# Encoder layer on one core: the first sequence's matrix-memory blocks are turned by VectorE and a DRAM buffer instead of by TensorE

## The chip, the core and the metric

The program runs on one core of a Trainium2 chip. The metric is the device time of one execution in microseconds (us). Five engines work side by side, each through its own instructions strictly in the order in which they stand: TensorE (PE, with PEld for its weight loads), VectorE (DVE), ScalarE (ACT), GpSimd (POOL) and SyncE (SP). DMA transfers are issued by instructions that stand in the queue of SP, POOL or ACT, and an instruction that waits holds up everything behind it on its engine.

## The reference, cut to what matters

Two sequences of 512 tokens (`x_prompt`, here s = 0, and `x_sample`, s = 1) go through the same layer: a half-step SwiGLU feed-forward, a mixing block, a second feed-forward, a final norm. In the mixing block a grouped-query attention (8 heads) and a bidirectional matrix memory (4 heads of width 128) run on the same normalised input:

```
att = gqa_block_attention(aq, ak, av)
mem = mlstm_bidirectional(mq, mk, mv, gate_pre, mlstm_gate_bias, o_pre, mlstm_head_norm)
merged = sigmoid(g_att) * (att @ w_up_att) + sigmoid(g_mlstm) * (mem @ w_up_mlstm)
x = x + merged @ w_out
```

Each direction of the memory computes, per head, weights from the gates, multiplies them with the scores `q k`, divides by the larger of the row sum's magnitude and `exp(-m)`, and applies the result to `v`; the two directions are added, normalised per head and gated.

## The kernel before, in words

Everything is kept transposed (128 channels on the partitions, 512 tokens along the row). Products are made in float32 precision from two parts of each operand: `split` writes a rounded high part (ACT, L733) and the rest (DVE, L734), and a product is three passes (high x high, high x low, low x high). Weights are split in the same way when they are first used: `load_w` fetches a raw tile `wr` (SP queue, L277), ACT writes the high part `w` (L284), DVE the low part (L285), and SP stores both into DRAM (`wpark`, L309). The second sequence loads the parked parts (L299) and splits nothing.

`mix(s, ...)` is the mixing block; both sequences run it one after the other, with parts interleaved. Units of work are pairs (load, compute), and `go` issues a unit's load one unit (s = 0) or two units (s = 1) ahead of the oldest one held. A scheduler then places the instructions on each engine by priority and by its own estimate of when each could run; `pin` keeps an instruction in program order, and `mark` pins the last matmul of a unit while `marks[0]` is set. So the order on an engine is not the order of the source.

The places the change and the prediction touch:

- Attention's end: `score` (L1118), softmax, `turn_keys` (PE transposes, L1134) or `fetch` of turned blocks from DRAM, `values` (L1165). Products of other units stand between them on PE.
- `mem_values`: the projection of the memory's `v` (96 products of 512 columns, L821), from four weight tiles, into the three banks `mm` and the bank `pso`.
- `mem_rows(h, d)`: loads the gate row of head h and direction d, spread over all partitions, into a quarter-tile `eb` of the tile `box` (L1088), and adds the mask to it to make `em` (L1091).
- `mem_head(h)`: four score products (L1309; the banks `pss`, two of them), 20 exponentials of 128x128 on ACT (L1323), DVE's product with row sums (L1325), the reciprocal `dn` (L1329 to L1331), and the normalisation (ACT L1336, DVE L1337 and L1339).
- `mem_out(h, ...)`: the four normalised tiles have to be turned so that they can be multiplied with `v` (L1381). The second sequence does this without PE: `mem_blocks` turns 32x32 blocks on DVE (L1347; eight instructions a head into two tiles `qt`), `mem_send` writes them to the DRAM buffer `tbuf` in eight DMAs on POOL's queue (L1355), and `mem_out` reads four tiles `f` back (L1368). The first sequence turns them by PE: 16 transposes of 128x128 a head (L1372) into the banks `pst`. Behind the product comes the head's norm (`block_sums`, `block_rstd` with its PE product L238, `spread_rows`).
- `merge_att(d)` (products with `w_up_att`), `mem_gate(d)`, `att_gate(d)` (gate projections): the units that stand between the heads.
- Small pools: four raw weight tiles `wr`, four row tiles `f2` (names `f`), eleven tiles `t2` (names `t`).

Of the kernel before, what the change touches and what calls it, by code (L numbers as in the profile page):

```python
# [8 lines left out]
F32 = mybir.dt.float32  # L9
# [3 lines left out]
ALU = mybir.AluOpType  # L13
# [3 lines left out]
P = 128  # L17
S = 512
D = 1024
KD = D // P  # L20
# [6 lines left out]
def encoder(ctx, tc, I, outs):  # L27
    nc = tc.nc
# [3 lines left out]
    wpool = ctx.enter_context(tc.tile_pool(name="wpool", bufs=3))  # L32
# [9 lines left out]
    def nm(s):  # L42
        n_id[0] += 1
        return f"{s}_{n_id[0]}"
# [269 lines left out]
    V_ = nc.vector  # L314
    G_ = nc.gpsimd
# [422 lines left out]
    HM, DM = 4, 128  # L738
# [8 lines left out]
    tabs = []  # L747
# [39 lines left out]
    marks = [False]  # L787
# [4 lines left out]
    def go(*units):  # L792
        for load, comp in units:
            held.append((comp, load()))
            while len(held) > ahead[0]:
                c, w = held.pop(0)
                c(w)
# [65 lines left out]
    EARLY = 6  # L863

    def mix(s, xh, xl, early=None, extra=None, after=None):
# [3 lines left out]
        queue = []  # L869

        def fill(n):
            go(*queue[:n])
            del queue[:n]

        def F2(dtype=F32):
            return T2(dtype, "f2")
# [52 lines left out]
        mg = A([P, KD, S], F32, "mg")  # L929
# [39 lines left out]
        ebuf = dpool.tile([2, 4, HM, P], F32, name=nm("ebuf"))  # L969
# [52 lines left out]
        def mem_values():  # L1022
            def done(pvv):
                vm = A([P, 2, 4, S], F32R, "Vm")
                for b in range(4):
                    nc.scalar.activation(vm[:, 0, b, :], pvv[b], AF.Copy, scale=rcol(b))
                    rest(vm[:, 1, b, :], pvv[b], b, f(vm[:, 0, b, :]))
                Vm.append(vm)
            return tok_proj(xh, xl, [(1792, 512)], 2, done, (MM, MM, MM, PO))
# [3 lines left out]
        def mem_qk(h, j):  # L1033
            def done(pp):
                if j == 0 and not s:
                    t = wpool.tile([P, 4, S], F32R, tag="w8", bufs=4, name=nm("qk"))
                    qks[h] = [t[:, i] for i in range(4)]
                elif s:
                    t = mem[:, 2 + j] if h == 2 else wpool.tile([P, 2, S], F32R, tag="wr", bufs=4, name=nm("qk"))
                    qks.setdefault(h, []).extend(t[:, i] for i in range(2))  # L1040
                t = pp
                if not s:
                    t = F2()
                    V_.tensor_tensor(t, pp, R[s], op=ALU.mult)
                split(t, *qks[h][2 * j:2 * j + 2])
            return win_cols((768, 1280)[j] + h * P, done)
# [10 lines left out]
        def att_gate(d):  # L1057
            def done(pp):
                gate_of(mg[:, d, :], pp)
            return win_cols(2832 + d * P, done)  # L1060
# [23 lines left out]
        def mem_rows(h, d):  # L1084

            eb = T2(F32, "eb")
            eb3 = eb.rearrange("p (b s) -> p b s", b=4)
            nc.sync.dma_start(eb3, ebuf[d, :, h, :].partition_broadcast(P))  # L1088
            em = T2(F32, "eb")
            em3 = em.rearrange("p (b s) -> p b s", b=4)  # L1090
            (V_ if s or not h else G_).tensor_tensor(em3, eb3, tabs[3][:, d].unsqueeze(1).to_broadcast([P, 4, P]), op=ALU.add)  # L1091
            return eb3, em3

        def mem_scales():
# [178 lines left out]
        def merge_att(d):  # L1273
            def done(pu):
                V_.scalar_tensor_tensor(mg[:, d, :], mg[:, d, :], 1.0, pu, op0=ALU.add, op1=ALU.mult)
            return up_unit(0, d, att, done)
# [3 lines left out]
        def mem_gate(d):  # L1280
            def done(pp):
                t = ths[d] = T2()
                gate_of(t, pp)
            return win_cols(3856 + d * P, done)
# [56 lines left out]

        def mem_blocks(h, Ts):

            q = [wpool.tile([P, 8, 4, 32], F32, tag="wr", bufs=4, name=nm("qt")) for _ in range(2)]
            for i in range(4):
                for g in range(2):
                    V_.transpose(q[g][:, :, i, :],  # L1347
                                 Ts[i][0][:, g * 256:(g + 1) * 256].rearrange("p (n m) -> p n m", m=32))
            return h, q

        def mem_send(h, q):

            for g in range(2):
                for a in range(4):
                    mark(nc.gpsimd.dma_start(tbuf[h % 2][8 * g:8 * g + 8, :, a, :].rearrange("n r x -> r n x"),  # L1355
                                      q[g][32 * a:32 * a + 32].rearrange("r n i m -> r n (i m)")), True)
            return h % 2

        def mem_out(h, Ts):
            moved = isinstance(Ts, int)  # L1360
            vm = Vm[0]
            po = PO()
            hs_ = slice(h * P, (h + 1) * P)
            turned = []
            for j in range(4 + 1):
                if j < 4 and moved:
                    p = F2()
                    mark(nc.gpsimd.dma_start(p, tbuf[Ts][4 * j:4 * j + 4].rearrange("c r a x -> (c r) (a x)")), True)  # L1368
                elif j < 4:
                    p = PT()  # L1370
                    for i in range(4):
                        nc.tensor.transpose(p[:, i * P:(i + 1) * P], Ts[i][0][:, j * P:(j + 1) * P], ident)  # L1372
                if j < 4:
                    ph, pl = T2(F32R), T2(F32R)
                    split(p, ph, pl)
                    turned.append((j, ph, pl))
                if j >= 1:
                    t, ph, pl = turned.pop(0)
                    with shifted(15):
                        for n, (a, b) in enumerate(((0, ph), (1, ph), (0, pl))):  # L1380
                            mark(nc.tensor.matmul(po, vm[:, a, t, hs_], b, start=(t == 0 and n == 0),  # L1381
                                                  stop=(t == 3 and n == 2)), True)
            h2 = T2()
            og = ogs[h]
            if moved:
                rows_ = T2()
                nc.scalar.activation(rows_.rearrange("p (i a m) -> p i a m", i=4, a=4),
                                     po.rearrange("p (a i m) -> p i a m", i=4, a=4), AF.Copy)
                po = rows_
            nc.scalar.activation(h2, po, AF.Square)  # L1390
            V_.scalar_tensor_tensor(og, og, 1.0, po, op0=ALU.add, op1=ALU.mult)
            turned_ = own[0] if own else F2()
            row = block_sums(h2, turned_)
            with shifted(60):
                rh = block_rstd(row, DM)
            with shifted(160):
                Rh = spread_rows(rh, turned_)
                V_.scalar_tensor_tensor(og, og, hn[:, h:h + 1], Rh, op0=ALU.mult, op1=ALU.mult)
                split(og, mem[:, h, 0, :], mem[:, h, 1, :])

        if s:
            qk2, qk3 = [[mem_qk(h, j) for j in range(2)] for h in (2, 3)]
            ma = [merge_att(d) for d in range(KD)]
            marks[0] = True
            q = mem_blocks(0, mem_head(0))
            at = [mem_send(*q)]
            go(*mem_values(), *qk2)
            q = mem_blocks(1, mem_head(1))
            go(*qk3, ma[0], ma[1])
            mem_out(0, at[0])  # L1410
            at.append(mem_send(*q))
            q = mem_blocks(2, mem_head(2))
            go(att_gate(6), att_gate(7), ma[2], ma[3])
            mem_out(1, at[1])
            at.append(mem_send(*q))
            q = mem_blocks(3, mem_head(3))
            go(*ma[4:])
            mem_out(2, at[2])
            at.append(mem_send(*q))
            go(*[mem_gate(d) for d in range(EARLY)])  # L1420
            mem_out(3, at[3])
            marks[0] = False
        for h in range(HM if not s else 0):
            Ts = mem_head(h)
            if h == 0:
                go(*mem_values())
            queue.append(merge_att(2 * h))
            if h == 0:
                queue.append(merge_att(1))
            fill(1 + s)  # L1430
            mem_out(h, Ts)
            if h + 2 < HM:
                queue.extend([att_gate(h + 6), mem_qk(h + 2, 0), mem_qk(h + 2, 1)])
            if h:
                queue.append(merge_att(2 * h + 1))
            fill(99)

        mh, ml = A([P, KD, S], F32R, "mh"), A([P, KD, S], F32R, "ml")
        go(*[mem_gate(d) for d in range(EARLY * s, KD)])
        go(*[merge_mem(d) for d in range(KD)])  # L1440
        flush()
        yield None
# [553 lines left out]
```

## Time and profile before

| what | value |
|---|---|
| time, median of 3 runs (lowest to highest) | 2029.29 us (2028.79 to 2030.15) |
| the profiled execution's own time | 2029.24 us |
| its span in the profile | 2027.5 us |
| PE busy | 2015.1 us, 99% |
| DVE, ACT, POOL busy | 1592.6, 919.2, 249.7 us (79%, 45%, 12%) |
| first sequence's attention tail, memory and merge | about 788 to 985 us from the span's start |
| second sequence's | about 1150 to 1340 us |

The span is the profiled part of the execution; the 1.7 us by which the execution's time exceeds it lie outside. An engine's share counts the time in which at least one of its instructions runs. The share of a whole span is an average; the stage from 788 us on is the one to read here.

### The profile page before, as it was taken

The numbers are of one execution on the slowest core, as the hardware profiler recorded it, in microseconds if no ns is written. First come the engines' busy times: TensorE is split into PE (matmuls) and PEld (weight loads), VectorE is DVE, ScalarE is ACT, GpSimd is POOL, SyncE is SP. The second block draws the span as 40 slices with busy tenths as digits, with TensorE's granted clock in tenths as the row PEclk, the third lists the DMA queues.
The fourth block names the chain that finished last, engine by engine and source line by source line (L and its number), as shares of the span: only waits on it lengthen the run. The fifth ranks groups of instructions, "written<-read, shape, count | busy, mean of one in ns | idle before, by whom it ended". The sixth has DMA issues, their size and how long they took to land.

```text
span 2027.5 us, 26874 instructions
## 1 busy us (share of the span) xinstructions
PE 2015.1 (99%) x9129; PEld 1661.4 (82%) x9129; DVE 1592.6 (79%) x2830; ACT 919.2 (45%) x1677; POOL 249.7 (12%) x313
## 2 busy tenths in 40 slices
PE   9999999999999999999999999999999999999998
PEld 7888888888888888788888878888888888888887
DVE  8989898896688788786566867377798988786797
ACT  7644444443224477653325655245444444442224
POOL 0243344201003000100120023011000000000001
PEclk9999999999999999999999999999999999999999
DMA  9778787799766766868657668867565655699753
GB/s 313 233 235 271 228 279 244 258 337 373 264 220 220 274 194 198 267 206 300 210 165 220 205 228 264 274 208 238 157 210 171 226 168 178 204 339 349 272 194 120
DMA packets 329546, 482.11 MB, mean 238 GB/s; under 512 B 23016, under 2 KB 196160, under 8 KB 328128
## 3 DMA queue, kind: packets, MB, share of 16 engines
q1 hardware_dynamic: 316352, 439.27, 64.9%
q0 software_dynamic: 12896, 40.86, 5.9%
q8 instruction: 72, 1.18, 0.2%
q14 instruction: 66, 0.54, 0.1%
q10 hardware_dynamic: 160, 0.27, 0.0%
HBM read 308.70 MB, written 171.61 MB: 237 GB/s over the span
## 4 chain that ended last, share of the span: by engine, by line
PE 94%; DVE 2%; DMA 2%; issue 1%; ACT 1%; SPq 0%; DVEq 0%; ACTq 0%
PE mm L856 16%; PE mm L380 11%; PE pso L380 11%; PE pst L380 11%; PE mm L650 9%; PE mm L842 5%; PE pss L380 5%; PE pss L650 4%; PE pst L650 4%; PE mm L821 3%; PE pso L650 3%; PE pss L1118 1%; PE pso L1165 1%; PE pso L1381 1%; PE pst L856 1%; PE pss L856 1%
## 5 line engine op out<-in xcount | busy, mean ns | idle before, releaser
L380 PE MATMUL pst<-xc,w 128*128 128x512 f32 x1056 | 253.8, 389 | 0.5 <-ACT t L415 0.5
L380 PEld LDWEIGHTS pst<-xc,w 128*128 128x128 f32 x1056 | 198.1, 188 | 42.0 <-ACT t L415 0.9
L380 PE MATMUL mm<-xc,w 128*128 128x512 f32 x972 | 229.8, 390 | 0.8 <-ACT t L388 0.8
L380 PEld LDWEIGHTS mm<-xc,w 128*128 128x128 f32 x972 | 181.8, 188 | 39.5 <-ACT t L388 1.9
L650 PE MATMUL mm<-rt,w 128*128 128x512 f32 x765 | 178.7, 389 | 0.0
L856 PE MATMUL mm<-xh,w 128*128 128x512 f32 x560 | 176.0, 391 | 0.0
L650 PEld LDWEIGHTS mm<-rt,w 128*128 128x128 f32 x765 | 143.5, 188 | 29.8
L338 ACT ACTIVATE w<-t 128x512 fp32r<-128x512 f32 x176 | 107.6, 628 | 130.7 <-issue 59.1
L339 DVE TENSOR_TENSOR w<-t,w 128x512 fp32r<-128x512 f32 x176 | 120.2, 701 | 31.7 <-ACT w L338 30.0
L380 PE MATMUL pso<-xc,f 128*128 128x512 f32 x528 | 127.1, 390 | 0.1
L380 PE MATMUL pss<-xc,w 128*128 128x512 f32 x528 | 126.8, 389 | 0.0
L380 PE MATMUL pso<-xc,w 128*128 128x512 f32 x528 | 126.8, 389 | 0.0
L856 PEld LDWEIGHTS mm<-xh,w 128*128 128x128 f32 x560 | 104.9, 188 | 21.8
L380 PEld LDWEIGHTS pso<-xc,f 128*128 128x128 f32 x528 | 98.9, 188 | 21.5 <-DVE t L419 1.1
L380 PEld LDWEIGHTS pss<-xc,w 128*128 128x128 f32 x528 | 99.1, 188 | 20.6
L380 PEld LDWEIGHTS pso<-xc,w 128*128 128x128 f32 x528 | 99.1, 188 | 20.6
L842 PE MATMUL mm<-xh,w 128*128 128x512 f32 x336 | 110.5, 395 | 0.0
L856 PE MATMUL mm<-xl,w 128*128 128x512 f32 x280 | 109.6, 391 | 0.0
L733 ACT ACTIVATE w<-wr 128x512 fp32r<-128x512 f32 x72 | 45.1, 632 | 138.3 <-PE pso L650 70.6
L733 ACT ACTIVATE w<-t 128x512 fp32r<-128x512 f32 x82 | 51.8, 632 | 107.4 <-PE pst L650 62.4
L650 PE MATMUL pss<-rt,w 128*128 128x512 f32 x396 | 93.7, 389 | 0.0
L650 PE MATMUL pst<-rt,w 128*128 128x512 f32 x396 | 93.7, 389 | 0.0
(464 smaller groups left out, 4168.1 us busy)
## 6 DMA issues: line engine op xcount, KB each, us to landing
rt<-rbuf SPq DMA_DIRECT2D x154, 512.0 KB, 5.8
w<-wpark SPq DMA_DIRECT2D x112, 512.0 KB, 5.1
wpark<-w SPq DMA_DIRECT2D x64, 512.0 KB, 3.6
wr<-in_ffn_w_gate_dram SPq DMA_DIRECT2D x62, 512.0 KB, 5.5
wr<-in_ffn_w_up_dram SPq DMA_DIRECT2D x44, 512.0 KB, 4.8
rbuf<-f SPq DMA_DIRECT2D x86, 256.0 KB, 4.3
rbuf<-R SPq DMA_DIRECT2D x82, 256.0 KB, 4.7
rbuf<-tab SPq DMA_DIRECT2D x74, 256.0 KB, 3.9
```

The costliest lines, as they stand in the source:

```text
L338: pin(nc.scalar.activation(t[:, 0], src, AF.Copy))
L339: pin(V_.tensor_tensor(t[:, 1], src, f(t[:, 0]), op=ALU.subtract))
L380: nc.tensor.matmul(p, a[:, k, :], xt[:, b, k, :], start=(first and k == 0 and i == 0), stop=(k == HK_ - 1 and i == 2), skip_group_check=True)
L650: nc.tensor.matmul(p, u[:, a, d * P:(d + 1) * P], r[:, b, ts], start=(first and q == 0 and k == 0), stop=(q == len(us) - 1 and k == 2), sk ...
L733: nc.scalar.activation(hi, src, AF.Copy)
L821: mark(nc.tensor.matmul(p[b][:, :N], a[:, k, bs], w_[:, kl, :], start=(k == 0 and i == 0), stop=(k == KD - 1 and i == 2)), (kl, b, i) == ( ...
L842: pin(nc.tensor.matmul(p[0], a[:, k, :], b, start=(k == 0 and i == 0), stop=(k == n - 1 and i == 2)))
L856: mark(nc.tensor.matmul(p, a[:, k, :], b, start=(k == 0 and i == 0), stop=last), last)
L1118: pin(nc.tensor.matmul(p, qT[:, h, b * P:(b + 1) * P], kv[:, hk * 2 + j, :], start=(j == 0), stop=(j == 1)))
L1165: pin(nc.tensor.matmul(pos[h], Vst[:, kb, h // 4, :], w, start=(kb == KBS[0] and i == 0), stop=(kb == KBS[3] and i == 1)))
L1381: mark(nc.tensor.matmul(po, vm[:, a, t, hs_], b, start=(t == 0 and n == 0), stop=(t == 3 and n == 2)), True)
```

## The change

The first sequence now follows the second's program: `mem_blocks`, `mem_send` and the reading `mem_out` for both, with the units between the heads given in one list. Its blocks go into one raw weight tile and into a quarter of the attention gates' tile (`mg[:, 6:8]`), because it needs the other raw weight tiles for its weights. All additions of the mask (L1091) are DVE's, where POOL had the first sequence's heads 1 to 3, and the first sequence's gate rows are loaded from ACT's queue instead of SP's. The norm's second row tile is the one that the memory's product was copied to (`po`), not a tile `f2`.

```
-            nc.sync.dma_start(eb3, ebuf[d, :, h, :].partition_broadcast(P))
+            (nc.sync if s else nc.scalar).dma_start(eb3, ebuf[d, :, h, :].partition_broadcast(P))
...
-            (V_ if s or not h else G_).tensor_tensor(em3, eb3, tabs[3][:, d].unsqueeze(1).to_broadcast([P, 4, P]), op=ALU.add)
+            V_.tensor_tensor(em3, eb3, tabs[3][:, d].unsqueeze(1).to_broadcast([P, 4, P]), op=ALU.add)
...
-            q = [wpool.tile([P, 8, 4, 32], F32, tag="wr", bufs=4, name=nm("qt")) for _ in range(2)]
+            q = [wpool.tile([P, 8, 4, 32], F32, tag="wr", bufs=4, name=nm("qt")) for _ in range(1 + s)]
+            if not s:
+                q.append(mg[:, 6:8].rearrange("p a (n i m) -> p (a n) i m", i=4, m=32))
...
-            turned_ = own[0] if own else F2()
+            turned_ = own[0] if own else po
...
+        qk2, qk3 = [[mem_qk(h, j) for j in range(2)] for h in (2, 3)]
+        ma = [merge_att(d) for d in range(KD)]
+        marks[0] = True
+        q = mem_blocks(0, mem_head(0))
+        at = [mem_send(*q)]
+        go(*mem_values(), *qk2)
+        q = mem_blocks(1, mem_head(1))
+        go(*qk3, ma[0], ma[1])
+        mem_out(0, at[0])
+        at.append(mem_send(*q))
+        q = mem_blocks(2, mem_head(2))
+        go(*([att_gate(6), att_gate(7), ma[2], ma[3]] if s else ma[2:6]))
+        mem_out(1, at[1])
+        at.append(mem_send(*q))
+        q = mem_blocks(3, mem_head(3))
+        mgs = [mem_gate(d) for d in range(KD)]
         if s:
...
+        else:
+            go(*mgs[:2])
+            at.append(mem_send(*q))
+            mem_out(2, at[2])
+            go(att_gate(6), att_gate(7), ma[6], ma[7], *mgs[2:4])
+        mem_out(3, at[3])
+        marks[0] = False
-        for h in range(HM if not s else 0):
-            Ts = mem_head(h)
-            if h == 0:
-                go(*mem_values())
-            queue.append(merge_att(2 * h))
-            if h == 0:
-                queue.append(merge_att(1))
-            fill(1 + s)
-            mem_out(h, Ts)
-            if h + 2 < HM:
-                queue.extend([att_gate(h + 6), mem_qk(h + 2, 0), mem_qk(h + 2, 1)])
-            if h:
-                queue.append(merge_att(2 * h + 1))
-            fill(99)
```

The second sequence's instructions stand as before on every engine. In the first sequence they move. Line numbers of the kernel after are higher by two from `mem_blocks` on and, behind the list of units, lower by six (the turns L1347 are L1349, the reads L1368 are L1370, the product L1381 is L1383).

PE at the end of the first sequence's attention, before. L1165 are attention's value products, L821 the products of `mem_values`, L1309 the memory's scores (`pss_7086` and `pss_7099` are the last two of head 0, `pss_7463` belongs to head 1):

```order
L1165 MATMUL pso_7007<-t_701_7015,kv_5410 128x512
L821 MATMUL mm_7143<-w_7136,xh_5029 128x512
L821 MATMUL mm_7143<-w_7136,xl_5030 128x512
L1165 MATMUL pso_7007<-t_702_7016,kv_5410 128x512
L1165 MATMUL pso_7007<-t_704_7026,kv_5410 128x512
L821 MATMUL mm_7144<-w_7136,xh_5029 128x512 x2
L1165 MATMUL pso_7007<-t_705_7027,kv_5410 128x512
L821 MATMUL mm_7144<-w_7136,xl_5030 128x512
L1309 MATMUL pss_7086<-qk_5811 128x512 x3
L821 MATMUL pso_7145<-w_7128,xh_5029 128x512 x2
```

The same place after (`pss_7335` and `pss_7348` are head 1's first two):

```order
L1165 MATMUL pso_7007<-t_701_7015,kv_5410 128x512
L1165 MATMUL pso_7007<-t_702_7016,kv_5410 128x512
L1165 MATMUL pso_7007<-t_704_7026,kv_5410 128x512
L1165 MATMUL pso_7007<-t_705_7027,kv_5410 128x512
L1309 MATMUL pss_7086<-qk_5811 128x512 x3
L1309 MATMUL pss_7099<-qk_5811 128x512 x3
L1309 MATMUL pss_7335<-qk_5940 128x512 x3
L1309 MATMUL pss_7348<-qk_5940 128x512 x3
L821 MATMUL mm_7159<-w_7145,xh_5029 128x512
```

Before, 35 of the 96 products of `mem_values` stand ahead of attention's last value product; after, none does, and all 96 stand behind four scores in a row.

DVE behind head 0's scores, before. L285 are low parts of weights (`w_7172` and `w_7204` are the last two tiles of `mem_values`, the first two stand further up; `w_7236` is `w_up_att`'s first), L1337 and L1339 the normalisation:

```order
L285 TENSOR_TENSOR w_7172<-wr_7170,w_7172 128x1024
L1325 SCALAR_TENSOR_TENSOR t_719_7103,dn_7059<-pss_7099,t_719_7103 128x512
L1325 SCALAR_TENSOR_TENSOR t_720_7109,dn_7059<-pss_7099,t_720_7109 128x128
L1329 SCALAR_TENSOR_TENSOR dn_7059<-dn_7059 128x8
L1330 TENSOR_TENSOR dn_7059<-dn_7059,st_5417 128x8
L285 TENSOR_TENSOR w_7204<-wr_7202,w_7204 128x1024
L1331 RECIPROCAL dn_7059<-dn_7059 128x8
L285 TENSOR_TENSOR w_7236<-wr_7234,w_7236 128x1024
```

The same place after, from head 0's last normalisation on (`w_7145` is the first tile of `mem_values`; L1091 makes head 1's two masked rows):

```order
L1337 SCALAR_TENSOR_TENSOR t_719_7103<-t_720_7109,dn_7059,t_719_7103 128x128
L1349 STREAM_TRANSPOSE qt_7126<-t_713_7077 128x8x32
L1349 STREAM_TRANSPOSE mg_5414<-t_713_7077 128x8x32
L1349 STREAM_TRANSPOSE qt_7126<-t_716_7090 128x8x32
L1349 STREAM_TRANSPOSE mg_5414<-t_716_7090 128x8x32
L1349 STREAM_TRANSPOSE qt_7126<-t_719_7103 128x8x32
L1349 STREAM_TRANSPOSE mg_5414<-t_719_7103 128x8x32
L1091 TENSOR_TENSOR box_5409<-box_5409,tab_4349 128x512 x2
L285 TENSOR_TENSOR w_7145<-wr_7143,w_7145 128x1024
```

The first low part of `mem_values` has moved behind all of head 0's scores, normalisation and turns, and behind head 1's masked rows, whose gate rows are loaded once head 0's exponentials have left their place in `box`.

ACT in attention's tail, after. The issue of head 0's first gate row (L1088) has come into this queue between two splits of attention; in the kernel before it stands on SP, behind the last write of attention's turned blocks:

```order
L1126 ACTIVATE t_680_6951<-t_680_6951,asm_6949 128x512
L733 ACTIVATE t_682_6960<-pst_6955 128x512
L1088 DMA box_5409<-ebuf_5416 128x4x128
L733 ACTIVATE t_686_6969<-f_685_6967 128x512
L733 ACTIVATE t_689_6977<-f_688_6975 128x512
```

DVE behind head 3's scores, before: `w_8152`, `w_8188` and `w_8224` are weights of the units that follow, and stand among the head's own work:

```order
L1325 SCALAR_TENSOR_TENSOR t_871_7999,dn_7949<-pss_7989,t_871_7999 128x128
L246 TENSOR_TENSOR row_7910<-row_7910 128x16
L285 TENSOR_TENSOR w_8152<-wr_8150,w_8152 128x1024
L247 SCALAR_TENSOR_TENSOR row_7910<-row_7910 128x16
L1329 SCALAR_TENSOR_TENSOR dn_7949<-dn_7949 128x8
L285 TENSOR_TENSOR w_8188<-wr_8186,w_8188 128x1024
```

The same place after: `w_7912` is the weight of the first `mem_gate`, the next unit on PE, and stands behind the head's eight turns and head 1's norm (L264, L1400):

```order
L1349 STREAM_TRANSPOSE mg_5414<-t_845_7865 128x8x32
L1349 STREAM_TRANSPOSE qt_7901<-t_848_7878 128x8x32
L1349 STREAM_TRANSPOSE mg_5414<-t_848_7878 128x8x32
L264 STREAM_TRANSPOSE t_834_7797<-row_7801 128x512
L1400 SCALAR_TENSOR_TENSOR box_5409<-box_5409,hn,t_834_7797 128x512
L285 TENSOR_TENSOR w_7912<-wr_7910,w_7912 128x1024
```

The weight's low part has moved from among the head's sums to behind its last turn.

More of the change, by code (lines that the diff above doesn't have):

```diff
@@ L1399, in mem_out @@
                 split(og, mem[:, h, 0, :], mem[:, h, 1, :])
-        if s:
[L1402 to L1416, printed above, removed]
+        qk2, qk3 = [[mem_qk(h, j) for j in range(2)] for h in (2, 3)]
[14 more added lines that the diff above has]
+        mgs = [mem_gate(d) for d in range(KD)]
+        if s:
             go(*ma[4:])
@@ L1419, in mix @@
             at.append(mem_send(*q))
-            go(*[mem_gate(d) for d in range(EARLY)])
-            mem_out(3, at[3])
-            marks[0] = False
-        for h in range(HM if not s else 0):
-            Ts = mem_head(h)
-            if h == 0:
-                go(*mem_values())
-            queue.append(merge_att(2 * h))
-            if h == 0:
-                queue.append(merge_att(1))
-            fill(1 + s)
-            mem_out(h, Ts)
-            if h + 2 < HM:
-                queue.extend([att_gate(h + 6), mem_qk(h + 2, 0), mem_qk(h + 2, 1)])
-            if h:
-                queue.append(merge_att(2 * h + 1))
-            fill(99)
+            go(*mgs[:EARLY])
+        else:
[5 more added lines that the diff above has]
+        marks[0] = False
         mh, ml = A([P, KD, S], F32R, "mh"), A([P, KD, S], F32R, "ml")
-        go(*[mem_gate(d) for d in range(EARLY * s, KD)])
+        go(*mgs[EARLY if s else 4:])
         go(*[merge_mem(d) for d in range(KD)])
```

## The prediction, made before the changed kernel was run

> **What bounds the kernel now.** I read the page's busy times and the shares of the chain that ended last, then the busy time in two windows: the first sequence's memory, which changes, and the second's, which already runs the program that the first is to get.
>
> ```profile
> PE 2015.1 (99%) x9129; PEld 1661.4 (82%) x9129; DVE 1592.6 (79%) x2830; ACT 919.2 (45%) x1677; POOL 249.7 (12%) x313
> PE 94%; DVE 2%; DMA 2%; issue 1%; ACT 1%; SPq 0%; DVEq 0%; ACTq 0%
> 788.00:925.00 137.00, 135.90 (x638) 109.52 (x637) 109.54 (x259) 85.67 (x183) 9.28 (x8) 1.00 0.72 238
> 1160.00:1300.00 140.00, 139.26 (x617) 112.78 (x616) 89.69 (x257) 66.31 (x161) 29.45 (x52) 1.00 0.78 259
> 922.68 32.55 PE mm L856 x143
> ```
>
> In the windows the columns are the stretch's length, then busy time with instructions of PE, PEld, DVE, ACT and POOL, the granted clock, DMA share and GB/s. PE is the bound: it idles 137.00 - 135.90 = 1.1 us of the first window and 0.74 us of the second, and carries 94% of the chain. DVE has 27 us free in the first window. So work taken from PE is worth its full price, and any wait put on PE costs its full length; there is no slack to absorb it. The row of the chain gives a product's pace: 32.55 / 143 = 0.227 us. The question is whether PE still finds its operands in time in the new order.
>
> **What the change removes from PE.** The 64 transposes.
>
> ```profile
> 759.88 0.60 PE L1134 MATMUL pst<-ident,t 128*128 128x128 f32 x4
> 760.24 0.48 PE L842 MATMUL mm<-xh,w 128*128 128x512 f32 x1
> 760.55 0.39 PE L842 MATMUL mm<-xl,w 128*128 128x512 f32 x1
> L1372 PE MATMUL pst<-ident,t x64: 270/272/328, 828.3 to 916.2; 128*128 128x128 f32 x64
> ```
>
> A lone transpose lasts 0.27 us, but they are pipelined. Four of them and the product behind stand between 759.88 and 760.55; less one product's pace, 0.227, a group of four costs about 0.44 us. 16 groups: **-7.0 us**. The most that all the waits of PE in that window can give back on top is the 1.1 us it idles: **-1.1**.
>
> **What it adds off PE.** DVE gets 32 block turns and six mask additions, POOL's queue 32 sends and 16 reads, ACT's queue eight loads of gate rows and ACT four copies.
>
> ```profile
> 1192.12 2.07 DVE L1347 STREAM_TRANSPOSE qt<-t 128x256 f32<-128x256 f32 x6
> L1091 DVE TENSOR_TENSOR box<-box,tab 128x512 f32<-128x512 f32 x7 | 4.8, 689 | 6.0 <-DMA box<-ebuf 5.9
> L1387 ACT ACTIVATE t<-pso 128x512 f32<-128x512 f32 x4 | 2.4, 598 | 7.5 <-PE pso L1381 7.5
> L1355 POOL DMA_DIRECT2D tbuf<-qt x32 | 18.6, 589 | 52.6 <-DVE qt L1347 51.6 <-DVE Vm L883 1.0
> L1368 POOL DMA_DIRECT2D f<-tbuf x16 | 8.7, 550 | 19.3 <-DMA tbuf<-qt 12.1 <-DVE row L232 3.9 <-ACT t L1323 3.1
> f<-tbuf POOLq DMA_DIRECT2D x16, 256.0 KB, 5.8
> ```
>
> Six turns take 2.07 us, so 32 take 11; six additions 4.1. 15 us fit into DVE's 27 free ones, the 2.4 us of copies into ACT's 51, 27 us of issues into POOL's 128. The round trip through DRAM (eight sends at 0.59 us, landing, a read of 5.8 us) is covered for three heads by the units between send and product; I take **C = 2** us (0 to 4) for the one whose last tile `f` must wait for a slot held by a unit of the queue. Behind a read that waits on POOL's queue stand only later reads and sends of the memory; behind a gate row's issue on ACT stand splits and exponentials, which is counted in A. By throughput the change would be a gain. By order it is not.
>
> **Wait A: attention's end.** Before, 35 products of `mem_values` fill PE while ACT and DVE make head 0's exponentials. After, all 96 stand behind four scores, and their first weight's low part behind head 0's normalisation, turns and head 1's masked rows on DVE.
>
> ```profile
> 811.20 0.39 PE L1165 MATMUL pso<-t,kv 128*128 128x512 f32 x1
> 799.41 0.59 ACT L733 ACTIVATE t<-pst 128x512 fp32r<-128x512 f32 x1
> 795.97 0.38 SPq L1088 DMA_DIRECT2D box<-ebuf  x1
> box<-ebuf SPq DMA_DIRECT2D x7, 256.0 KB, 6.0
> 810.19 1.56 ACT L1323 ACTIVATE t<-box,st 128x128 f32<-128x128 f32 x5
> 816.80 1.55 ACT L1323 ACTIVATE t<-box,st 128x128 f32<-128x128 f32 x5
> 1184.40 3.90 ACT L1323 ACTIVATE t<-box,st 128x128 f32<-128x128 f32 x13
> 1188.98 0.17 DVE L1329 SCALAR_TENSOR_TENSOR dn<-dn 128x8 f32<-128x8 f32 x1
> 1196.24 0.69 DVE L1091 TENSOR_TENSOR box<-box,tab 128x512 f32<-128x512 f32 x1 [2.04 <-DMA box<-ebuf]
> 1197.57 0.69 DVE L1091 TENSOR_TENSOR box<-box,tab 128x512 f32<-128x512 f32 x1
> L285 DVE TENSOR_TENSOR w<-wr,w 128x1024 fp32r<-128x1024 f32 x25 | 32.4, 1296 | 6.2 <-ACT w L284 6.1
> ```
>
> Times here are on the clock of before. PE runs dry after attention's last product (811.4), less the 35 products that went away (7.9), plus the six score products for which its two banks are free (1.4): 804.9. The first gate row now leaves from ACT's queue behind the split after the one at 799.41, so about 801, and lands 6 us later, 807; before, SP issued it at 795.97. Its mask addition stands on DVE ahead of five splits of attention, so these are late too and the exponentials start about 812 (808 to 814; before, 810.19). Twenty of them ran from 810.19 to 818.35 before with a score between; I take 7.4: 819.4. In the second sequence, from the last exponential's end (1188.30) through normalisation and turns to the end of the next head's second masked row (1198.26) it took 10.0 us, 2.04 of them for the gate row's landing, which is to be waited for here too: 829.4. The low part takes 1.3: 830.7. From 804.9 that is 25.8, less the other six score products (1.4) that run inside: **A = 24** (19, where the exponentials start at 808 and the gate row is there, to 28).
>
> **Waits B to G: the same three times more.** From `dn` (1188.98) to the last turn (1192.12 + 2.07) DVE needs 5.2 us a head, and the next unit's weight again stands behind that.
>
> ```profile
> L734 DVE TENSOR_TENSOR t<-pst,t 128x512 fp32r<-128x512 f32 x23 | 15.2, 685 | 5.9 <-ACT t L733 5.9
> L264 DVE STREAM_TRANSPOSE f<-row 128x512 f32<-128x512 f32 x4 | 2.9, 712 | 0.1
> L246 DVE TENSOR_TENSOR row<-row 128x16 f32<-128x16 f32 x12 | 2.1, 174 | 0.3
> L1398 DVE SCALAR_TENSOR_TENSOR box<-box,hn,f 128x512 f32<-128x512 f32 x4 | 4.1, 1030 | 0.1
> L1323 ACT ACTIVATE t<-box,st 128x128 f32<-128x128 f32 x80 | 24.3, 390 | 1.8 <-POOL box L1091 1.8
> PE pss L1309 <- DVE t L1325: 1.7, 3, 0.7
> ```
>
> - B, head 1: about 1.0 for the last scores' row sums, 5.2, an eviction (0.7) and the low part (1.3) make 8.2 us; PE has 24 products, 5.4. **2.7** (1 to 4).
> - D, the scores of heads 2 and 3 stand four in a row, with two banks: the third waits for ten exponentials (10 x 0.39 = 3.9) and a row sum (0.7), less its own 0.7: **4** (3 to 5.5). In the page's waits this cost 1.7 us in the whole run.
> - E, `w_7689` behind head 2: 5.2, two splits (1.4), L264 (0.7), the low part (1.3) and some of the norm's small steps (0.17 each, 0.8 together), less 1.4 of scores: **8** (6.5 to 10).
> - F, head 3's last scores wait for exponentials that the norm's copy of head 1 holds back: **1.8** (1 to 3), half of ten exponentials.
> - G, `w_7912` behind head 3: row sum 1.0, 5.2, small steps 1, L264 0.7, L1398 (L1400 after) 1.0, low part 1.3, with next to nothing left for PE: **10** (8 to 13).
>
> **PE after a long wait.** The only pause of PE in before that is long is the one ahead of its first products.
>
> ```profile
> 1.63 2.93 PE L1468 MATMUL pst<-xc 128*128 128x512 f32 x6 [1.63 <-DVE xc L1553]
> L1468 PE MATMUL pst<-xc x9: 628/628/797, 1.6 to 8.8; 128*128 128x512 f32 x9
> ```
>
> Those six took 2.93 us where six at 0.227 take 1.4; such a product lasts 0.63 us instead of 0.39. A, E and G are waits of the kind; three times 1.5 is **4.5** (0 if a pause of this length costs nothing, 9 if twice). [...] The granted clock in the windows above reads 1.00, with no pause in them, so before can't show it.
>
> **Sum.** Waits: 24 + 2.7 + 2 + 4 + 8 + 1.8 + 10 = 52.5 (38.5 to 67.5). The profiled execution took 2029.24 us (span 2027.5 and 1.74 outside; the median of the runs is 0.05 above it). 2029.24 - 7.0 - 1.1 + 52.5 + 4.5 = **2078 us**. Its own range: 2021.1 + 38.5 + 0 = 2060 to 2021.1 + 67.5 + 9 = 2098.
>
> **Rivals.**
> - R1, the gain, and the other side: the second sequence runs the same units with 0.74 us of idle PE in 140. If the low parts are ready whenever PE asks, the time is 2021 us. It decides at waits of 8.1 us in all. Against it: in wait A alone DVE's own work behind the last exponential is 7.9 us (5.2 of normalisation and turns, 1.4 of masked rows, 1.3 of low part), and twenty exponentials stand before that, with 1.4 us of scores for PE; the second sequence loads parked parts and has no low part to make.
> - R2, only A is real: from B on, weights and scores catch up, because DVE, once ahead of a PE that starts 24 us late, has these units' raw tiles already there. 2021.1 + 19 to 28 + 1.5: 2042 to 2051. For it speaks that DVE has time in the window; against, that the order on DVE is fixed and puts the splits behind the turns whatever time there is.
> - R3, PE stays slow for long after the waits, since D, E, F and G follow one another within some 80 us of products and hardly leave a long busy stretch. A third of these at half pace adds 25 us to the sum without the 4.5: 2099; half of them, 2115. For it, only the slow first products; against, the granted clock of 1.00 around the short pauses of before. [...]
>
> **How the numbers follow.** The sum as forecast 0.70, R2 0.12, R3 0.09, R1 0.07, unnamed 0.02. The time is the sum's, 2078. The range goes to 2042, so that R2 is in and R1 out, and to 2102, where the sum's upper end and R3's lower lie; outside it are R1, two thirds of R3 and the rest, some 0.17 with the sum's tails. 0.2%, 4 us, is about what a measurement of this kernel can tell from no change. Of R1 0.05 is faster and 0.02 lies where the waits just cancel the gain; all others are slower, 0.93.
>
> **What would show it.** PE's idle time in the first sequence's stage goes from 1 us to near 50, in one piece of over 18 us behind attention's last product that ends with the low part of `mem_values`' first weight, and in two of 6 to 13 us that end with the low parts behind head 2's and head 3's turns. The turns should last 0.35 us each, POOL's reads end none of PE's waits over 4 us, and the first products after the long waits show durations over 0.39 us. The second sequence keeps its times, shifted. I am wrong if PE waits under 30 us in the stage, which would mean that splits come earlier than my walk of DVE's order, or if products stay slow for tens of microseconds.

## The result, and the profile after

The changed kernel takes 2081.77 us (median of four runs, 2079.78 to 2083.19), the kernel before on the same chip 2029.72: a ratio of 1.0256 (1.0240 to 1.0272), 52 us slower. The profiled execution took 2082.33 us, its span is 2080.6.

The page of the changed kernel, busy times and the shares of the chain that ended last:

```profile
PE 2029.5 (98%) x9065; PEld 1665.2 (80%) x9065; DVE 1605.0 (77%) x2868; ACT 923.0 (44%) x1681; POOL 270.5 (13%) x355
...
PE 91%; DVE 3%; DMA 3%; ACT 2%; SPq 1%; issue 1%; DVEq 0%; ACTq 0%; POOLq 0%
```

PE has 64 instructions less and is busy 14 us longer. The first products of `w_up_mlstm`, the same point of the program, start at 955.07 us in before and at 1009.19 after; at 788 both stand within about 1 us of each other. So the whole loss, some 54 us, lies in this stretch. The windows of before and then of the changed kernel (length, PE busy, PEld, DVE, ACT, POOL, granted clock, DMA share, GB/s):

```profile
788.00:955.07 167.07, 165.97 (x770) 134.41 (x769) 126.19 (x283) 94.64 (x194) 9.28 (x8) 1.00 0.76 256
```

```profile
788.00:1009.19 221.19, 181.35 (x700) 138.13 (x699) 137.29 (x319) 97.19 (x195) 28.34 (x50) 0.88 0.74 236
798.00:805.00 7.00, 4.66 (x19) 2.77 (x19) 4.45 (x9) 4.60 (x10) 0.00 (x0) 1.00 0.38 138
806.00:809.00 3.00, 3.00 (x12) 2.41 (x12) 0.87 (x2) 0.60 (x1) 0.00 (x0) 0.50 0.00 0
847.00:850.00 3.00, 3.00 (x8) 2.32 (x8) 1.91 (x2) 0.84 (x1) 0.00 (x0) 0.50 0.89 350
866.00:872.00 6.00, 3.80 (x16) 2.75 (x16) 4.88 (x9) 1.58 (x2) 0.56 (x1) 1.00 0.57 219
```

PE's idle time goes from 1.1 to 39.8 us: +38.7. Busy time goes up by 15.4 although 7.0 us of transposes (the prediction's estimate) are gone: some **22.4 us are products that ran slow**, because the granted clock falls from 1.00 to 0.88 in the mean and to 0.50 in stretches, or that stood alone and overlapped with nothing (0.39 us for a product alone, 0.23 in a row). DVE is busy 137 of 221 us; it is not full.

What PE waited for in this stretch, the five largest (engine, line, releaser; total, times, longest):

```profile
PE mm L856 <- ACT w L284: 8.4, 2, 5.4
PE pso L1383 <- ACT t L733: 6.3, 2, 5.2
PE mm L821 <- DVE w L285: 5.4, 2, 3.3
PE mm L856 <- DVE w L285: 5.1, 2, 3.1
PE pss L1309 <- DVE t L1325: 3.9, 5, 2.2
```

The high (L284) and low parts (L285) of weights make up half of it. The places that the prediction calls A, E and G, in PE's timeline of the changed kernel:

```profile
810.70 0.50 PE L1165 MATMUL pso<-t,kv 128*128 128x512 f32 x1 [0.23 <-DVE t L734]
813.40 6.12 PE L1309 MATMUL pss<-qk 128*128 128x512 f32 x12 [2.20 <-DVE t L1325]
821.46 0.73 PE L821 MATMUL mm<-w,xh 128*128 128x512 f32 x2 [1.95 <-ACT w L284]
825.48 0.80 PE L821 MATMUL mm<-w,xh 128*128 128x512 f32 x1 [3.28 <-DVE w L285]
...
901.10 1.65 PE L856 MATMUL mm<-att,w 128*128 128x512 f32 x3 [2.93 <-ACT w L284]
904.75 9.35 PE L856 MATMUL mm<-att,w 128*128 128x512 f32 x33 [2.00 <-DVE w L285]
...
928.47 0.79 PE L856 MATMUL mm<-xh,w 128*128 128x512 f32 x1 [5.43 <-ACT w L284]
...
932.78 1.22 PE L856 MATMUL mm<-xh,w 128*128 128x512 f32 x2 [3.10 <-DVE w L285]
```

Behind attention's last product, PE has twelve scores and two products to do in 14.3 us. DVE's timeline shows head 0's first masked row and then the release of A, the low part directly behind turns and masked rows. The raw weight had long been there: SP loaded it at 792.45.

```profile
802.35 0.69 DVE L1091 TENSOR_TENSOR box<-box,tab 128x512 f32<-128x512 f32 x1 [0.99 <-DMA box<-ebuf]
...
822.71 0.40 DVE L1349 STREAM_TRANSPOSE mg<-t 128x256 f32<-128x256 f32 x1
823.03 1.25 DVE L1091 TENSOR_TENSOR box<-box,tab 128x512 f32<-128x512 f32 x2
824.20 1.22 DVE L285 TENSOR_TENSOR w<-wr,w 128x1024 fp32r<-128x1024 f32 x1
```

```profile
792.45 1.52 SPq L277 DMA_DIRECT2D wr<-in_w_in_dram  x3
821.43 11.47 SPq L309 DMA_DIRECT2D wpark<-w  x6
833.00 5.82 SPq L277 DMA_DIRECT2D wr<-in_w_in_dram  x3
```

SP's rows carry the clue to why the weights come so late: loads now come mostly in groups of three, each behind the stores of the three before. In before, all four loads of `mem_values` stood ahead of 690 us:

```profile
678.05 2.79 SPq L277 DMA_DIRECT2D wr<-in_w_in_dram  x4
```

### The profile page after: what moved, and what is told of

It reads as the page before. It is cut to its first block, busy times and chain, and to the rows that moved or that the text cites. A ratio compares the mean times of both kernels' runs of the same rounds, so it can differ in the third digit from the quotient of the medians.

```text
span 2080.6 us, 26880 instructions
## 1 busy us (share of the span) xinstructions
PE 2029.5 (98%) x9065; PEld 1665.2 (80%) x9065; DVE 1605.0 (77%) x2868; ACT 923.0 (44%) x1681; POOL 270.5 (13%) x355
## 4 chain that ended last, share of the span: by engine, by line
PE 91%; DVE 3%; DMA 3%; ACT 2%; SPq 1%; issue 1%; DVEq 0%; ACTq 0%; POOLq 0%
PE mm L856 14%; PE pso L380 11%; PE pst L380 11%; PE mm L380 10%; PE mm L650 8%; PE pss L380 6%; PE mm L842 5%; PE pst L650 4%; PE pss L650 4%; PE mm L821 3%; PE pso L650 3%; PE pss L1118 1%; PE pso L1165 1%; PE pso L1383 1%; PE pst L856 1%; PE pss L856 1%
```

## The experiments

**Why the order is as it is.** The changed kernel takes, for each head, a new tile of the four raw weight tiles for its turned blocks. My theory: tiles of such a pool are given out in program order, so the scheduler places a load whose tile was taken later only once the head's turns are placed; the ring, not the turns' work, sets the order. The rival: the turns' own work on DVE, POOL's queue and DRAM is what PE waits for.

*One tile for all heads* (the first taken at head 0):

```
-            q = [wpool.tile([P, 8, 4, 32], F32, tag="wr", bufs=4, name=nm("qt")) for _ in range(1 + s)]
+            q = [wpool.tile([P, 8, 4, 32], F32, tag="wr", bufs=4, name=nm("qt")) for _ in range(2 * s)]
             if not s:
+                if not qts:
+                    qts.append(wpool.tile([P, 8, 4, 32], F32, tag="wr", bufs=4, name=nm("qt")))
+                q.append(qts[0])
```

> The changed kernel with one raw weight tile taken once for the turned blocks of all four heads, instead of a new one from the four for each head. Theory (the order): a new block tile for each head stands in the ring of the raw weight tiles ahead of the weights that follow it in the program, so these are loaded and split only behind the head's turns; with one tile kept, the weights of heads 1 to 3 come in front of the turns again, while head 0's still come behind. The wait at attention's end stays (about 27 us of idle and slow PE up to 866 us), the later ones (about 35 us behind 866) mostly go: 2047 to 2057 us. Rival (the turns' own work on DVE, POOL's queue and DRAM is what PE waits for): nothing of that work is taken away, so 2078 to 2085 us.

2065.42 us against 2027.91, 1.0187 (1.0172 to 1.0203).

*`mem_values` ahead of head 0* (a new tile per head as before):

```
+        if not s:
+            go(*mem_values())
         q = mem_blocks(0, mem_head(0))
         at = [mem_send(*q)]
-        go(*mem_values(), *qk2)
+        go(*(mem_values() if s else []), *qk2)
```

> The changed kernel with the units of mem_values written ahead of head 0 instead of behind its turns; a new block tile for each head as before. Theory (the order): 34 of the 96 products stand among attention's last ones again and their weights' low parts ahead of the turns, so the wait at attention's end goes (about 27 us), and the later ones stay (about 35 us): 2054 to 2064 us. Rival (the turns' own work): that work is the same, so the end of attention gains little and the time is 2074 to 2085 us.

2072.43 us, 1.0217 (1.0202 to 1.0233). *Both edits together*:

> Both edits together: mem_values ahead of head 0, and one raw weight tile kept for the turned blocks. All turns, sends, reads, mask additions on DVE and gate rows from ACT's queue are as in the changed kernel. Theory (the order): PE's idle time in the first sequence's stage falls from 40 us to under 6, its clock stays at 1.00, and the 64 transposes taken away show: 2022 to 2028 us, faster than the kernel before by 0.1 to 0.4%. Rival (the turns' own work): 2060 us or more. If the gate rows on ACT's queue or the masks on DVE cost something on the path, it shows here as 2028 to 2035 us.

2054.63 us, 1.0128 (1.0113 to 1.0143).

Of the changed kernel's 2.56%, the two edits take back 0.69, 0.39 and, together, 1.28%: half of the loss, without taking away one turn, send or read. In the order of instructions both do what the theory says: with `mem_values` first, 34 of its products stand among attention's last ones; with one tile, the next weights stand ahead of the turns of heads 1 to 3. But all three numbers missed: the second half stayed. The rival's missed too, by 13, 2 and 5 us on the fast side. PE's waits with both edits:

```profile
PE mm L856 <- DVE mg L889: 11.2, 1, 11.2
PE pso L1386 <- ACT t L733: 5.1, 4, 3.9
PE mm L856 <- ACT w L284: 5.0, 1, 5.0
PE mm L856 <- DVE w L285: 3.5, 2, 3.3
```

Wait A is gone; others had taken its place. Before hunting them I ran the reverse, *the kernel before with nothing but the tile*:

```
             Ts = mem_head(h)
+            t = wpool.tile([P, 8, 4, 32], F32, tag="wr", bufs=4, name=nm("qt"))
+            V_.transpose(t[:, :, 0, :], Ts[3][0][:, 0:256].rearrange("p (n m) -> p n m", m=32))
             if h == 0:
                 go(*mem_values())
```

> The kernel before, with its transposes on TensorE, and one thing added: for each head of the first sequence a raw weight tile is taken behind the normalisation and one block turn of 0.4 us is written to it, which nothing reads. Theory (the order): the taken tile alone moves the weights behind the normalisation, and the time goes to 2055 to 2085 us without any turn, DRAM trip, mask or gate row of the change. Rival (the turns' own work): four instructions of 0.4 us off the path leave 2029 to 2032 us.

2056.89 us, 1.0143 (1.0126 to 1.0160). Four instructions of 0.4 us, which nobody reads, cost 29 us, since they hold a place in the ring. Its SP queue shows how: the first gate rows, then the three raw loads that in before had long been issued. Room was not lacking: the weights loaded before had all been split by 675.5 us, and no raw tile was in use from then until these loads.

```profile
793.44 20.45 SPq L1088 DMA_DIRECT2D box<-ebuf  x3
813.93 1.53 SPq L277 DMA_DIRECT2D wr<-in_w_in_dram  x3
```

This shows the ring as a cause that suffices for 1.4 of the 2.56%.

**What held the second half.** With both edits, DVE's timeline has waits of two other kinds, and PE's 11.2 us end with the last row:

```profile
824.05 0.69 DVE L1091 TENSOR_TENSOR box<-box,tab 128x512 f32<-128x512 f32 x1 [6.34 <-DMA box<-ebuf]
...
848.05 0.69 DVE L1091 TENSOR_TENSOR box<-box,tab 128x512 f32<-128x512 f32 x1 [6.88 <-DMA box<-ebuf]
...
933.70 1.29 DVE L889 TENSOR_TENSOR mg<-mm,R 128x512 f32<-128x512 f32 x2 [6.76 <-DMA tbuf<-mg]
```

The mask addition waits on DVE for its gate row, with weights behind it; and `att_gate(6)` writes to the quarter of the gates' tile in which head 3's blocks still wait to be sent. *Masks of heads 1 to 3 back on POOL* (`(V_ if s or not h else G_).tensor_tensor(em3, ...)`):

> The kernel with both edits (values first, one block tile kept), and the mask additions of heads 1 to 3 back on POOL; gate rows stay on ACT's queue. In the trace of both edits DVE stood 6.3 and 6.9 us in a mask addition, waiting for the gate row's transfer, with the low parts of the next weights behind it; PE then waited 5.0 and 3.3 us and ran at a clock of 0.50 for some 10 us behind. Theory 2 (a mask addition on DVE puts the gate row's flight time in front of the weights): PE loses these 8 us and about 5 of slow clock no longer: 2054.6 - 13 = 2041 us (2037 to 2046). Rival (the wait merely moves, POOL's addition takes 1.4 us instead of 0.7 and holds up the sends behind it): 2050 to 2056 us.

2053.89 us, 1.0118 (1.0103 to 1.0133): nothing gained that can be told, and theory 2 (the mask on DVE costs the wait) fell as an explanation of this order. The wait moved to ACT, whose exponentials need the same masked row, and behind them on ACT stand the weights' high parts:

```profile
824.61 2.09 ACT L1323 ACTIVATE t<-box,st 128x128 f32<-128x128 f32 x6 [7.88 <-POOL box L1091]
```

*That, and `att_gate(6)`, `att_gate(7)`, `merge_att(6)`, `merge_att(7)` behind the last `mem_out`*:

```
-            go(att_gate(6), att_gate(7), ma[6], ma[7], *mgs[2:4])
+            go(*mgs[2:5])
...
-        go(*mgs[EARLY if s else 4:])
+        go(*([] if s else [att_gate(6), att_gate(7), ma[6], ma[7]]), *mgs[EARLY if s else 5:])
```

> As the run with the masks on POOL, and the units att_gate(6), att_gate(7), merge_att(6), merge_att(7) put behind the last mem_out, one mem_gate more ahead of it. In the trace of both edits PE stood 11.2 us because att_gate(6) writes the part of the gates' tile that holds head 3's turned blocks, whose transfer landed 12 us after its issue. Theory 3 (the borrowed quarter of the gates' tile costs this wait): 11 us and about 3 of slow clock go, and with little left to wait for the 64 transposes show: 2022 to 2031 us against 2028 of before. Rival (the same wait moves to the last head's product, which now has fewer products in front): 2036 to 2044 us.

2060.32 us, 1.0152 (1.0136 to 1.0167), 6 us slower. The wait for the gates' tile, 8.9 us in the run before it, went, and 12.0 us for head 2's turned tiles took its place. *The same, with gate rows from SP's queue again* (`nc.sync.dma_start(eb3, ...)`):

> As the run before it, and the gate rows issued by SP again. Theory (a gate row's place in a queue only matters through the wait of the mask addition, now on POOL): within 4 us of the run with the late gates. Rival (SP's queue stands 17 us in the stores of weight parts, so the rows come late there and the exponentials with them): 5 to 15 us slower than it.

2054.98 us, 1.0118 (1.0100 to 1.0136): 5 us faster than with ACT's queue, just outside what I expected, and the rival's sign was wrong. The waits at heads 1 and 2 are short now (none over 2 us). One long wait is left, and POOL's timeline names it: head 2's four reads stand behind head 3's eight sends, which wait for head 3's turns.

```profile
917.42 2.31 POOL L1360 DMA_DIRECT2D tbuf<-qt  x4 [18.82 <-DVE qt L1352]
919.72 2.31 POOL L1360 DMA_DIRECT2D tbuf<-mg  x4
923.44 2.21 POOL L1373 DMA_DIRECT2D f<-tbuf  x4 [1.41 <-DMA tbuf<-qt]
```

```profile
931.36 5.74 PE L1386 MATMUL pso<-t,Vm 128*128 128x512 f32 x12 [11.67 <-ACT t L733]
```

The changed kernel has this order too (its 5.2 us at L1383). *Head 2's reads ahead of head 3's sends, and one `mem_gate` more behind them*:

```
-            at.append(mem_send(*q))
             mem_out(2, at[2])
-            go(*mgs[2:5])
+            at.append(mem_send(*q))
+            go(*mgs[2:6])
```

> As the run with late gates and gate rows from SP, and the reads and products of mem_out for head 2 put ahead of head 3's sends, with one mem_gate more behind them. In that run's trace head 2's reads stood on POOL's queue behind head 3's sends, which wait for head 3's turns; PE waited 11.7 us for them and ran at 0.50 of its clock for about 10 us around it. Theory 4 (the order on POOL's queue makes this wait): 11.7 us and 4 to 6 of slow clock go: 2055 - 17 = 2038 us (2033 to 2042), still slower than before's 2028.6, since four waits of 1 to 2 us stay and each is followed by 3 to 5 us at half clock. Rival (the wait moves to head 3's product): 2046 to 2055 us.

2039.36 us, 1.0050 (1.0038 to 1.0063), as expected. The stretch up to the same point as in the first section is 177.56 us, PE idle in 13.9 of them:

```profile
788.00:965.56 177.56, 163.69 (x695) 128.71 (x694) 132.99 (x310) 96.90 (x193) 36.20 (x56) 0.97 0.85 284
```

No version beat the kernel before. But the last one keeps all turns, sends and reads of the change, so that their own work can account for no more than 0.50 of the 2.56%. It still pays 13.9 us of waits, none over 1.9 us, and some 4.7 of slow products (177.56 - 167.07 = 10.5 = 12.8 more idle - 7.0 + 4.7), more than the transposes' 7.0. Three raw tiles for weights where there were four is a candidate for the rest; that was not tried on its own.

**The other part of the change alone.** *The kernel before with gate rows from ACT's queue and all masks on DVE*:

> The kernel before with this one part of the change alone: gate rows from ACT's queue and all mask additions on DVE; transposes on TensorE, order of the units as before. Theory 2: DVE's queue takes in waits of 4 to 7 us for gate rows ahead of low parts, and PE, 99% busy, feels a part of them: 2030 to 2040 us against 2028. Rival (the mask's place costs nothing where a unit's products cover it): 2026 to 2029 us.

2034.14 us, 1.0028 (1.0018 to 1.0037): 5.5 us, a small cost of its own.

**The slow products.** *The changed kernel with the 64 transposes put back beside the turns, read by nobody*:

```
+            for j in range(4 * (not s)):
+                p = PT()
+                for i in range(4):
+                    nc.tensor.transpose(p[:, i * P:(i + 1) * P], Ts[i][0][:, j * P:(j + 1) * P], ident)
             return h, q
```

> The changed kernel with the 64 transposes on TensorE put back beside the block turns: each head's four tiles are also transposed into the banks pst, and nothing reads them. They stand on PE between each head's scores and the weights that it waits for. Theory (PE is idle there, and its clock falls to 0.50 when it stands much): 7.0 us more of work cost nothing, and the products behind each wait start at a higher clock: 2074 to 2082 us against 2082 of the changed kernel. Rival (the waits leave no room at these places): 2086 to 2090 us.

2080.70 us, 1.0253 (1.0239 to 1.0268): no slower than the changed kernel's 1.0256. The 7.0 us that the change saves on PE are worth nothing there that can be told. Windows of the changed kernel, then of this one, around wait A:

```profile
811.00:830.00 19.00, 11.57 (x27) 7.22 (x27) 16.23 (x47) 15.13 (x41) 4.66 (x8) 0.64 0.46 129
```

```profile
811.00:830.00 19.00, 14.80 (x61) 10.43 (x62) 15.20 (x46) 14.96 (x41) 4.65 (x8) 0.91 0.57 159
```

With 16 useless transposes in the wait, the mean clock there is 0.91 instead of 0.64, and the products behind it start 0.23 us apart, not 0.43. Part of that is not the transposes' doing: they begin at 817.76 us, and here the clock was back before: nine scores took 4.20 us from 811.41 on, three more only 0.96 from 815.94 on. In the changed kernel all twelve took 6.12, and the clock was back only at 819.32 (worked out as in the last section). But behind them, up to 830 us, it did not fall again, as it did in the changed kernel at 822.74: the mean of 0.91 over 19.00 us leaves 3.4 us at 0.50, and the products from 823.49 on start 0.23 us apart. Up to the first products of `w_up_mlstm` PE idles 34.4 us instead of 39.8.

```profile
788.00:1007.18 219.18, 184.76 (x760) 141.79 (x758) 136.59 (x317) 97.05 (x194) 28.30 (x50) 0.92 0.74 237
```

## Why the prediction was right, and which of its terms were not

The time, 2081.77 us, lies 4 us from the 2078 forecast. The mechanism held: the loss is made by the order, not by throughput, and the waits A, E and G end with weights behind head 0's, 2's and 3's turns. That the number came out so close is luck: two terms missed by 13 and 18 us in opposite directions.

- **Waits: too large by 13 us.** 52.5 forecast, 39.8 measured. Most of the miss is A: 24 forecast, 7.4 measured, in three pieces of which the longest is 3.3, and not in the one piece of over 18 us that was to show it. The low part was to be ready at 830.7, it was at 825.4. The gate row landed 3.5 us after its issue (799 to 802.4), not 6; the exponentials ended at 817.2, not 819.4; head 1's masked rows waited for nothing. On the other side attention's last product did not move forward by 7.9 us, as the walk had it: without the 35 products among them, attention's own products waited for their splits and evictions in pieces of up to 1.2 us (4.9 us from 788 to 811). And the twelve scores behind it took 6.1 us at a clock of 0.50, where 2.8 were counted. E was 4.9 of idle instead of 8, G 8.5 instead of 10, B 2.2 for 2.7, D and F 0.8 each for 4 and 1.8. Three waits that the sum did not name fill up a part: the 4.9 ahead of A, 2.6 at `mem_values`' last products (844 to 847 us) and 5.2 at head 2's product.
- **Slow PE: too small by 18 us, and outside its own bounds (0 to 9).** "Three times 1.5" counted a restart after each long wait. The trace shows stretches of 3.4 us and more at a clock of 0.50 behind far shorter waits: at 806 us, after 7 us in which PE was busy two thirds of the time and never stood over 1.1 us; at 847 after waits of 0.5 and 2.1 us; not at 868.7, after a wait of 2.2 us amid full work. There are seven such stretches, 54.6 us together, the two longest of 13.7 us, around E and G. This is the mechanism of R3, and nearly its lower price: 22.4 us measured, 25 named. (That price and the other one, for half of the products, do not fit together: by the first, half adds 37 us and gives 2111, not 2115.) The prediction was to be wrong if products stayed slow for tens of microseconds; taken together they did. With the waits as forecast and this price the sum would have given 2096.
- **C: wrong place.** A read held up by a tile `f` was to cost 2 us at one head; at head 0, whose reads waited so, 1.2 were measured. The read that cost 5.2 us was head 2's, behind head 3's sends on POOL's queue, an order that I had called harmless ("only later reads and sends of the memory"); by the prediction's own sign POOL's reads were to end no wait over 4 us.
- **The gain of 7.0 us:** the transposes left PE and were worth nothing in the changed order, as the run that put them back shows (2080.70 us against 2081.77). Beside 39.8 us of waits the saving did not count.
- The prediction took the order as given. That a tile of the ring had made much of it, it did not see; the runs showed it.
- R1 and R2 did not come about: PE idled 39.8 us, and 24.9 of them behind 866 us, where R2 had none.

## What to carry to other kernels

Where a pool's tiles are given out in program order, one tile borrowed for another purpose stands in front of every later load of that pool: look in the new order for loads that now come behind the borrower, before pricing the work moved. On a bound engine count, beside each new wait, the slow products behind it: here 22.4 us beside 39.8 of idle, and 4.7 beside 13.9 in the last version. And repair by the trace, one wait at a time, expecting each to hand over to the next: gate row, gates' tile and POOL's queue did here. Of six edits the first two took the loss from 2.56 to 1.28%, the next three left it at 1.18, and the last took it to 0.50.

## What was not expected of the hardware

In the changed kernel the granted clock falls to 0.50 without any long pause (at 806 us none over 1.1 us stood ahead of it), and the times of its changes lie near multiples of one step apart. Windows of 1 us in which it changes:

```profile
805.00:806.00 1.00, 0.40 (x1) 0.40 (x2) 1.00 (x2) 0.45 (x1) 0.00 (x0) 0.84 0.00 0
809.00:810.00 1.00, 0.78 (x5) 0.34 (x3) 0.05 (x2) 0.68 (x2) 0.00 (x0) 0.96 0.00 0
812.00:813.00 1.00, 0.00 (x0) 0.00 (x0) 0.97 (x2) 1.00 (x4) 0.00 (x0) 0.75 0.03 8
819.00:820.00 1.00, 0.52 (x2) 0.00 (x0) 1.00 (x5) 1.00 (x3) 0.00 (x0) 0.84 0.58 171
822.00:823.00 1.00, 0.19 (x1) 0.00 (x0) 1.00 (x4) 0.00 (x0) 0.00 (x0) 0.87 0.77 307
829.00:830.00 1.00, 1.00 (x5) 0.77 (x4) 0.47 (x2) 1.00 (x4) 0.00 (x0) 0.72 0.87 250
```

A mean of 0.84 over a window that ends at 0.50 puts the fall 0.32 us before its end: at 805.68; the return, worked out in the same way, is at 809.08, and the next changes are at 812.50, 819.32, 822.74 and 829.56. The steps are 3.40, 3.42, 6.82, 3.42 and 6.82 us, near once or twice 3.41. The shortest of the seven stretches at 0.50 last 3.4 us (805.68 to 809.08, 846.64 to 850.04), the longest 13.7. They do not go with the length of a wait alone: behind waits of 0.7, 0.2 and 0.6 us (891 to 894 us) the clock fell at 894.4, and came back 13.7 us later, with E in between; behind one of 2.2 us (866.5 to 868.7) it did not fall. Nor do they go with PE's busy time in the 3.41 us around, 2.08 in the first case and 1.81 in the second (each window ends a whole number of such steps behind 829.56 us):

```profile
891.02:894.43 3.41, 2.08 (x8) 1.27 (x8) 3.33 (x12) 3.41 (x13) 1.06 (x2) 1.00 0.76 255
867.12:870.53 3.41, 1.81 (x8) 1.44 (x9) 3.41 (x5) 1.58 (x2) 0.51 (x1) 1.00 0.38 154
```

What decides it was not shown.
